# Two transformer blocks on one core: SBUF tiles moved to other offsets within rows of 512 bytes

## The chip, the cores and the metric

The kernel runs on one core of one Trainium2 chip. The metric is device time in microseconds (us) of one execution. The kernel before takes 1174.03 us, the median of two timed runs (1173.64 and 1174.42).

## What is computed

Two blocks over 256 tokens of 1024 features, in float32. The first has two layers (an NSA and a differential attention mixer, then a MoBA mixer, each followed by an MLP), the second an RG-LRU branch beside a forgetting attention, a gated merge and a gated FFN. Cut to the products that take nearly all of the time:

```python
x = x + mixer(rms_norm(x) @ w_in) @ w_out      # layers 0 and 1
x = x + act(rms_norm(x) @ mlp_w1) @ mlp_w2     # 1024 -> 4096 -> 1024
...
proj = h @ w_in_2                              # 1024 -> 7696
y_a = gelu(ga) * rg_lru(conv(xa)); y_b = forgetting_attention(q, k, v, f)
merged = sig(g_a) * (y_a @ w_proj_a) + sig(g_b) * (y_b @ w_proj_b)
x = x + rms_norm(merged @ w_out_2)
up = conv(rms_norm(x) @ w_up)                  # 1024 -> 6144
x = x + rms_norm((gelu(gate) * val) @ w_down)  # 3072 -> 1024
```

## The kernel before, in words

All weights stream in once, in chunks of 1 MB by SyncE's queue (`w_load`, three buffers `raw`). Each chunk holds two units of 128 x 1024. A unit is split into a high and a low part, both float32r: ScalarE writes `whi` (L220), VectorE `wlo` = raw - whi (L221), in six buffers each of the pool `wp` (tags `hi` and `lo`, 4096 bytes of a partition). Activations are split the same way (`gh`/`gl`, `oh`/`ol`, `hh`/`hl`, `yh`/`yl`). A product of 128 features by 256 tokens over one k-tile is then three matmuls (`mm3`, L262 to L264): whi by xh, whi by xl, wlo by xh. In them the weights are the stationary operand (128 columns of 4 bytes: 512 bytes of each partition) and the activations stream past (256 columns: 1024 bytes). Only `gen_nat` (L435 to L437) has the roles the other way round: 128 tokens of `gh` or `gl` stand, and 256 columns of `whi` or `wlo` stream. All these matmuls are 128x128 by 128x256.

Four generators give the order of the work: `gen_pair` (two column tiles over eight k-tiles, from `gh`/`gl`), `gen_nat`, `gen_half` (four k-tiles, from `oh`/`ol`) and `gen_deep` (16, 24 or 32 k-tiles in a row, from `yh` or `hh`). `weave` lays the attention and RG-LRU steps between them. The order is fixed at build time; it runs in program order on each engine.

Where a tile lies in SBUF follows from the order of the `tile()` calls: the pools `cp` (constants), `xp`, `np`, `rawp`, `wp` stand one after the other at the start of the memory, and the pools of a stage (`ap0`, `hp`, `ap1`, `mp`, `fp`, `ff`) on top of them, opened and closed as a stack. Addresses are padded to 32 bytes. As a row k of a streamed tile is 1024 bytes long and a row k of a weight unit 512 (or 1024), the address modulo 512 is the same for every k. Built, the two programs have these offsets (address modulo 512) for the operands of the float32r matmuls, "distance" being the streamed one minus the standing one, modulo 512:

| stage (streamed, standing) | matmuls | before: offsets, distance | after: offsets, distance |
|---|---|---|---|
| `gen_pair` (gh/gl, whi/wlo), the FFN's first product apart | 3744 | 384, 320: 64 | 256, 0: 256 |
| the FFN's first product `w_up` (gh/gl, whi/wlo) | 1152 | 384, 320: 64 | 256, 0: 256 |
| `gen_nat` (whi/wlo, gh/gl) | 528 | 320, 384: 448 | 0, 256: 256 |
| layer 0's output `gen_half` (oh/ol) | 192 | 416, 320: 96 | 0, 0: 0 |
| second product of both MLPs (hh/hl) | 1536 | 320, 320: 0 | 128, 0: 128 |
| layer 1's output (oh1/ol1) | 192 | 320, 320: 0 | 384, 0: 384 |
| `w_pa` (yh/yl) | 240 | 320, 320: 0 | 192, 0: 192 |
| `w_pb` (oh2/ol2) | 192 | 320, 320: 0 | 320, 0: 320 |
| the FFN's second product (hh2/hl2) | 576 | 320, 320: 0 | 0, 0: 0 |

Two small products have standing units of 24 and 16 columns (`gen_small`: NSA's gates and the forget logits, `gs` in the profile). In the second the k-th unit stands at offset 320 + 64 k modulo 512, and `gh`/`gl` stream at 384, so its distances go 64, 0, 448, 384, 320, 256, 192 and 128.

Of the kernel before, what the change touches and what calls it, by code (L numbers as in the profile page):

```python
# [7 lines left out]
F32 = mybir.dt.float32  # L8
# [50 lines left out]
def kernel(  # L59
# [29 lines left out]
    cp = ctx.enter_context(tc.tile_pool(name="cp", bufs=1))  # L89
    xp = ctx.enter_context(tc.tile_pool(name="xp", bufs=1))  # L90
    np_ = ctx.enter_context(tc.tile_pool(name="np", bufs=2))
    rawp = ctx.enter_context(tc.tile_pool(name="rawp", bufs=3))
    wp = ctx.enter_context(tc.tile_pool(name="wp", bufs=6))
# [8 lines left out]
    ones = cp.tile([128, 128], F32, name="ones")  # L102
    mhalf = cp.tile([128, 8], F32, name="mhalf")
    x = xp.tile([128, KT, T], F32, name="x")
    gh = xp.tile([128, KT, T], FR, name="gh")
    gl = xp.tile([128, KT, T], FR, name="gl")
# [14 lines left out]

# [1 line left out]
    chunks = []  # L123
# [47 lines left out]
    add_stream(w_dn, U8)  # L171

    W = Ctl()
    W.raw = []
# [54 lines left out]

    # orders of k for a start on two pairs at once: unit by unit for a few k, or k by k  # L230
    K422 = ((0, 1, 2, 3), (4, 5), (6, 7))
# [4 lines left out]
    def w_next(held=0):  # L236
        # held: units taken whose products are not yet issued
        while len(W.q) < min(1 + AHEAD, 6 - held):
            if not w_split():
                break  # L240
        return W.q.pop(0)
# [4 lines left out]

# [1 line left out]
    def bc(ap, n):  # L248
# [48 lines left out]
    class Norm:  # L297
        # sums of squares over the features; the last `tail` tiles go straight to the summing products
        def __init__(self, t1=3, t2=6, tail=0):
# [146 lines left out]
    def gen_deep(ntile, nu, xh, xl, evac, group=1):  # L446
        # the first `group` column tiles are worked on unit by unit
        def block(js):
            pss_ = {j: psg.tile([128, 2, T], F32, tag="g", name="g") for j in js}
            for u in range(nu):  # L450
                for j in js:
                    wh, wl, (nk, ncol) = w_next()
                    if j == ntile - 1 and u == nu - 1:
                        w_ahead(4)
                    for k in range(nk):
                        kk = u * nk + k
                        mm3(pss_[j][:, 0, :], wh[:, k, :], wl[:, k, :], xh[:, kk, :], xl[:, kk, :], kk == 0, kk == nu * nk - 1)
                        if k == nk // 2 - 1:
                            tick()
                            yield  # L460
                    if u == nu - 1:
                        evac(j, pss_[j][:, 0, :])
                    tick()
                    yield

        yield from block(range(group))
        for j in range(group, ntile):
            yield from block([j])
# [87 lines left out]

# [1 line left out]
    BT = 3  # L558
# [3 lines left out]
    def maps_gen(maps, ap):  # L562
# [5 lines left out]
        def A(n):  # L568
            if n % 2 == 0:
                # two heads side by side, on the upper and the lower rows of the array  # L570
                qs = []
                for i in (n, n + 1):
                    m = maps[i]
                    if m.get("pre"):
                        m["pre"]()
                    st[i] = pss.tile([128, 512], F32, tag="s", name="s")
                    qs.append((st[i], m["q"](), m["k"]()))
                for s, q, k in qs:
                    nc.tensor.matmul(out=s[:, 128:384], lhsT=q[:, 128:256], rhs=k, start=True, stop=True)  # L579
                for s, q, k in qs:  # L580
                    nc.tensor.matmul(out=s[:, 0:128], lhsT=q[:, 0:128], rhs=k[:, 0:128], start=True, stop=True)
            m, s = maps[n], st[n]
# [84 lines left out]
    def pv_cols(S, n, v0, v1, first):  # L667
        # value product of one head, feature-major: rows of head n % 2, pair n // 2
        def f(ps):
# [7 lines left out]

# [1 line left out]
    xv = xT.rearrange("k p t -> p k t")  # L679
# [14 lines left out]
    w_load()  # L694
    tb_t = cp.tile([33, 16], F32, name="tb_t")
    nc.vector.memset(tb_t[32:33, :], NEGB)
    nc.vector.memset(ones, 1.0)
    nc.vector.memset(mhalf, -0.5)
    warm = cp.tile([128, 8], F32, name="warm")
    nc.scalar.activation(out=warm, in_=mhalf, func=AF.Square)  # L700
    # the tensor engine's clock rises with use: keep it busy until the first weights are here
    wps = pst.tile([128, 512], F32, tag="t", name="wps")
# [24 lines left out]

# [1 line left out]
    bias_ctx = ExitStack()  # L729
# [49 lines left out]

# [1 line left out]
    A0 = ExitStack()  # L781
    ap0 = A0.enter_context(tc.tile_pool(name="a0", bufs=1))
    qT = ap0.tile([128, 4, T], F32, name="qT")
    ksT = ap0.tile([128, T], F32, name="ksT")
# [14 lines left out]
    nlam = ap0.tile([128, 1], F32, name="nlam")  # L799
    wcmp = [ap0.tile([128, 2048], F32, tag="e8", name="wcmp%d" % i, bufs=2) for i in range(2)]  # L800
    for i in range(2):
        nc.sync.dma_start(out=wcmp[i], in_=w_cmp[i])

    norm = Norm(*(4, 7))
# [89 lines left out]
    def compress_gen():  # L894
# [16 lines left out]
        yield  # L911
        # keys on rows 0..29, values on rows 64..93
        hz = ap0.tile([94, 128], F32, name="hz")
# [3 lines left out]
        hp = pss.tile([128, 512], F32, tag="s", name="hp")  # L917
# [32 lines left out]

    # position n of the head order (i, g) -> head g * 4 + i
    HORD = [(n % 2) * 4 + n // 2 for n in range(8)]
# [126 lines left out]

    # the first sums of squares, in tiles that are free so far  # L1080
    sqs = [qT[:, 0:2, :], qT[:, 2:4, :], kcd[:, :, 0:T], vcd[:, :, 0:T]]
# [7 lines left out]
    norm.tail = 3  # L1089
    sgain = cp.tile([128, 1], F32, name="sgain")  # L1090
    have = {}
# [57 lines left out]

# [1 line left out]
    def mlp(norm, gain_next, nrm, nrm2=None):  # L1151
        st = ExitStack()
        hp = st.enter_context(tc.tile_pool(name="hp", bufs=1))
        hh = hp.tile([128, 32, T], FR, name="hh")
        hl = hp.tile([128, 32, T], FR, name="hl")
# [17 lines left out]
    def log1pe(pool, z, n, pre):  # L1173
        # log(1 + exp(-|z|)) by 2 atanh(e / (2 + e)); returns the steps and the result
        e = pool.tile([128, n], F32, name=pre + "e")
# [26 lines left out]

# [1 line left out]
    A1 = ExitStack()  # L1204
    ap1 = A1.enter_context(tc.tile_pool(name="a1", bufs=1))
    rb8 = ap1.tile([128, T], F32, name="rb8")
    vn = ap1.tile([128, 2, D], F32, name="vn")
    oh = ap1.tile([128, KT, T], FR, name="oh1")
    ol = ap1.tile([128, KT, T], FR, name="ol1")
# [57 lines left out]
    )  # L1267
    nsp = cp.tile([128, 10], F32, name="nsp")
    psp = cp.tile([128, 10], F32, name="psp")
    hb = cp.tile([128, 20], F32, name="hb")  # L1270
    hm = cp.tile([128, 16], F32, name="hm")
    sp_steps, sp_q = log1pe(cp, V("lam"), 10, "sp")
# [18 lines left out]

# [1 line left out]
    gc = cp.tile([128, 8], F32, name="gc")  # L1293
    nc.vector.tensor_tensor(out=gc, in0=V("fin"), in1=V("pre2"), op=ALU.mult)
# [3 lines left out]
    M = ExitStack()  # L1298
    mp = M.enter_context(tc.tile_pool(name="mp", bufs=1))
    yh = mp.tile([128, 10, T], FR, name="yh")  # L1300
    yl = mp.tile([128, 10, T], FR, name="yl")
# [38 lines left out]

# [1 line left out]
    RG = ExitStack()  # L1342
# [56 lines left out]
    def rg_gen():  # L1399
        for half in range(2):  # L1400
# [5 lines left out]
            for o in range(5):  # L1406
# [3 lines left out]
                for m in range(2):  # L1410
                    # blocks off the diagonal reach at most half of the columns
                    nb = [(pi, slice(0, 64) if pi < o else slice(64, 128)) for pi in prs if pi != o]
# [32 lines left out]
    def evac_f(ps):  # L1445
# [14 lines left out]
        def st15():  # L1460
            # log_sigmoid(z) = min(z, 0) - log(1 + exp(-|z|))
            nc.vector.scalar_tensor_tensor(out=L.l, in0=zn, scalar=0.0, in1=L.l, op0=ALU.min, op1=ALU.subtract)
# [32 lines left out]

# [1 line left out]
    FA = ExitStack()  # L1497
    fp = FA.enter_context(tc.tile_pool(name="fp", bufs=1))
    oh = fp.tile([128, KT, T], FR, name="oh2")
    ol = fp.tile([128, KT, T], FR, name="ol2")  # L1500
# [75 lines left out]

# [1 line left out]
    PO = ExitStack()  # L1578
# [34 lines left out]

# [1 line left out]
    FF = ExitStack()  # L1615
# [83 lines left out]

# [1 line left out]
def _pack(w, groups):  # L1701
# [226 lines left out]
```

## Time and profile before

| | us |
|---|---|
| median of the timed runs | 1174.03 |
| the profiled execution, first to last instruction (its span) | 1170.4 |
| left around the span, as median minus span | 3.7 |
| TensorE busy in the span | 1138.5 (97%) |
| VectorE busy | 793.4 (68%) |
| ScalarE busy | 625.7 (53%) |

The float32r matmuls above are 8352 of the 9343 matmul records. The time that the profile gives for one matmul (some 280 ns) is from its start to the end of its passage through the array, and follows overlap: what a matmul costs in a row of them is the distance from its start to the next one's start. That is read from the timeline, or from a stretch of known length and the number of matmuls in it (the count includes the two or three that are still under way as the stretch opens). The weight load of the next matmul runs during the present one.

### The profile page before, as it was taken

Reading aid. Unit: us, or ns where it says so; the run is one execution under the profiler, and the core shown is the slowest. Engines: PE = TensorE matmul, PEld = TensorE weight load, DVE = VectorE, ACT = ScalarE, POOL = GpSimd, SP = SyncE. Lnnn points to the kernel's source line nnn. Section 1 sums busy time; section 2 is a strip of 40 time slices with the busy share of each in tenths; the row PEclk is TensorE's granted clock in tenths of the full one; section 3 lists DMA queues with packets and bytes.
Section 4 is the critical chain, followed back from the end, with each engine's and each line's share of the span. In section 5 each row is a group of like instructions: output and inputs, shape, how many; then the busy total and the mean of one; then the engine's idle time right before and its main releaser. Section 6 shows DMA issues by size and latency. Waiting matters only on the chain.

```text
span 1170.4 us, 22694 instructions
## 1 busy us (share of the span) xinstructions
PE 1138.5 (97%) x9343; PEld 1088.1 (93%) x9343; DVE 793.4 (68%) x1404; ACT 625.7 (53%) x1112; POOL 190.3 (16%) x228
## 2 busy tenths in 40 slices
PE   8999999999999999999999999999999999999996
PEld 7987799999999889999999897999999999999996
DVE  5767766674545777566445787766567689999842
ACT  4346555653444545565434577644454556676641
POOL 2014320000010123000001000042310123222211
PEclk9999999999999999999999999999999989999998
DMA  8832244555444334355455453564555525445641
GB/s 331 290 136 73 74 180 145 212 202 199 177 184 180 141 113 145 144 214 206 158 215 198 153 204 109 175 239 141 166 180 197 173 99 167 164 175 180 212 149 36
DMA packets 31303, 200.01 MB, mean 171 GB/s; under 512 B 3594, under 2 KB 6042, under 8 KB 9056
## 3 DMA queue, kind: packets, MB, share of 16 engines
q1 hardware_dynamic: 28832, 187.23, 44.6%
q0 software_dynamic: 2080, 11.08, 2.9%
q8 instruction: 73, 1.20, 0.4%
q14 instruction: 30, 0.25, 0.1%
q10 hardware_dynamic: 288, 0.26, 0.1%
HBM read 197.43 MB, written 3.22 MB: 171 GB/s over the span
## 4 chain that ended last, share of the span: by engine, by line
PE 78%; DVE 14%; ACT 3%; issue 2%; POOL 2%; DMA 1%; SPq 0%; POOLq 0%; ACTq 0%
PE g L262 22%; PE g L264 21%; PE g L263 21%; DVE y L1643 4%; DVE wlo L221 4%; PE rgp L1414 2%; PE g L435 2%; PE g L436 2%; PE g L437 2%; PE pt L623 1%; PE o L673 1%; DVE u L1631 1%; ACT whi L220 1%; PE s L579 1%; DVE y L1655 1%
## 5 line engine op out<-in xcount | busy, mean ns | idle before, releaser
L221 DVE TENSOR_TENSOR wlo<-raw,whi 128x1024 fp32r<-128x1024 f32 (+2 forms) x356 | 420.3, 1212 | 114.2 <-ACT whi L220 113.9
L262 PE MATMUL g<-gh,whi 128*128 128x256 f32 x1632 | 463.7, 284 | 3.2 <-ACT whi L220 1.7
L264 PE MATMUL g<-gh,wlo 128*128 128x256 f32 x1632 | 460.1, 282 | 3.1 <-DVE wlo L221 3.1
L263 PE MATMUL g<-gl,whi 128*128 128x256 f32 x1632 | 457.6, 280 | 0.5 <-DVE gl L257 0.4
L220 ACT CAST whi<-raw 128x1024 fp32r<-128x1024 f32 (+2 forms) x356 | 349.9, 1024 | 18.0 <-PE g L263 8.4
L262 PEld LDWEIGHTS g<-gh,whi 128*128 128x128 f32 x1632 | 309.1, 189 | 10.6 <-issue 5.4
L264 PEld LDWEIGHTS g<-gh,wlo 128*128 128x128 f32 x1632 | 309.2, 189 | 7.2 <-DVE wlo L221 7.1
L263 PEld LDWEIGHTS g<-gl,whi 128*128 128x128 f32 x1632 | 309.4, 190 | 1.1 <-DVE gl L257 0.7
L262 PE MATMUL g<-hh,whi 128*128 128x256 f32 x704 | 199.4, 283 | 1.3 <-DVE u L1631 1.3
L264 PE MATMUL g<-hh,wlo 128*128 128x256 f32 x704 | 199.3, 283 | 0.2 <-DVE wlo L221 0.2
L263 PE MATMUL g<-hl,whi 128*128 128x256 f32 x704 | 199.2, 283 | 0.0
L262 PEld LDWEIGHTS g<-hh,whi 128*128 128x128 f32 x704 | 135.1, 192 | 1.5 <-ACT q L1652 1.5
L264 PEld LDWEIGHTS g<-hh,wlo 128*128 128x128 f32 x704 | 135.1, 192 | 0.4 <-DVE wlo L221 0.4
L263 PEld LDWEIGHTS g<-hl,whi 128*128 128x128 f32 x704 | 135.1, 192 | 0.0
L317 POOL TENSOR_TENSOR acc<-acc,sq 128x256 f32<-128x256 f32 x53 | 42.4, 806 | 465.2 <-ACT sq L313 464.3
L612 POOL TENSOR_TENSOR p<-p,rr 128x384 f32<-128x384 f32 x56 | 50.1, 895 | 205.9 <-DVE rr L607 92.8
L597 ACT ACTIVATE p<-p,nm 128x256 f32<-128x256 f32 x112 | 49.9, 448 | 56.0 <-DVE nm L588 55.8
L1643 DVE SCALAR_TENSOR_TENSOR y<-u,cw,y 128x255 f32<-128x255 f32 (+1 forms) x96 | 60.1, 685 | 0.0
L262 PE MATMUL g<-oh,whi 128*128 128x256 f32 x192 | 55.6, 290 | 0.0
L264 PE MATMUL g<-oh,wlo 128*128 128x256 f32 x192 | 54.3, 283 | 0.0
L263 PE MATMUL g<-ol,whi 128*128 128x256 f32 x192 | 54.2, 282 | 0.0
L1160 ACT ACTIVATE u<-u 128x512 f32<-128x512 f32 x32 | 20.2, 632 | 61.9 <-DVE u L1159 61.9
(317 smaller groups left out, 1455.8 us busy)
## 6 DMA issues: line engine op xcount, KB each, us to landing
raw<-in_w_in_dram SPq DMA_DIRECT2D x30, 1024.0 KB, 4.9
raw<-in_w_up_dram SPq DMA_DIRECT2D x24, 1024.0 KB, 4.9
raw<-in_w_m1a_dram SPq DMA_DIRECT2D x16, 1024.0 KB, 4.8
raw<-in_w_m2a_dram SPq DMA_DIRECT2D x16, 1024.0 KB, 5.0
raw<-in_w_m1b_dram SPq DMA_DIRECT2D x16, 1024.0 KB, 4.9
raw<-in_w_m2b_dram SPq DMA_DIRECT2D x16, 1024.0 KB, 4.9
raw<-in_w_od_dram SPq DMA_DIRECT2D x12, 1024.0 KB, 4.8
raw<-in_w_dn_dram SPq DMA_DIRECT2D x12, 1024.0 KB, 4.8
```

The source lines that it names most:

```text
L220: nc.scalar.copy(out=hi[:, a:b], in_=t[:, off + a:off + b])
L221: nc.vector.tensor_tensor(out=lo[:, a:b], in0=t[:, off + a:off + b], in1=hi[:, a:b].bitcast(F32), op=ALU.subtract)
L262: nc.tensor.matmul(out=o, lhsT=wh, rhs=xh, start=start, stop=False, skip_group_check=skip)
L263: nc.tensor.matmul(out=o, lhsT=wh, rhs=xl, start=False, stop=False, skip_group_check=skip)
L264: nc.tensor.matmul(out=o, lhsT=wl, rhs=xh, start=False, stop=stop, skip_group_check=skip)
L317: nc.gpsimd.tensor_tensor(out=self.acc, in0=self.acc, in1=dst, op=ALU.add)
L435: nc.tensor.matmul(out=ps[:, b, :], lhsT=xh[:, k, bs], rhs=wh[:, k % 4, :], start=(k == 0), stop=False)
L436: nc.tensor.matmul(out=ps[:, b, :], lhsT=xh[:, k, bs], rhs=wl[:, k % 4, :], start=False, stop=False)
L437: nc.tensor.matmul(out=ps[:, b, :], lhsT=xl[:, k, bs], rhs=wh[:, k % 4, :], start=False, stop=(k == KT - 1))
L597: nc.scalar.activation(out=p[:, c0:c1], in_=p[:, c0:c1], func=AF.Exp, scale=-1.0, bias=nm[:, b:b + 1], accum_out=sm[:, b:b + 1],)
L612: nc.gpsimd.tensor_tensor(out=pv, in0=pv, in1=w, op=ALU.mult)
L1643: nc.vector.scalar_tensor_tensor(out=y[:, a, d:], in0=u[:, a, 0:T - d], scalar=cw[:, w, c:c + 1], in1=y[:, a, d:], op0=ALU.mult, op1=ALU.add)
```

## The change

Tiles move; nothing else does. A helper `pad` allocates a tile of n floats per partition that no instruction touches, and it is called at seven places (once per MLP in `mlp`), ahead of the tiles named in the diff. Eight small tiles of the pool `cp` and the two `wcmp` tiles are allocated earlier than they were, so that what follows them starts at the wanted offsets. Comments are taken out, which moves line numbers by up to 17 (L262 of before is L279 after). The programs have the same instructions, in the same order, on every engine; a few POOL instructions wait for other semaphores, of transfers that ended long before. The highest address in use goes from 227,200 to 228,096 bytes.

```diff
+    pads = []
+
+    def pad(pool, n):
+        pads.append(0)
+        pool.tile([128, n], F32, tag="pad%d" % len(pads), name="pad", bufs=1)
+
...
     mhalf = cp.tile([128, 8], F32, name="mhalf")
+    tb_t = cp.tile([33, 16], F32, name="tb_t")
+    warm = cp.tile([128, 8], F32, name="warm")
+    sgain = cp.tile([128, 1], F32, name="sgain")
+    nsp = cp.tile([128, 10], F32, name="nsp")
+    psp = cp.tile([128, 10], F32, name="psp")
+    hb = cp.tile([128, 20], F32, name="hb")
+    hm = cp.tile([128, 16], F32, name="hm")
+    gc = cp.tile([128, 8], F32, name="gc")
+    pad(xp, 32)
     x = xp.tile([128, KT, T], F32, name="x")
+    pad(xp, 64)
     gh = xp.tile([128, KT, T], FR, name="gh")
     gl = xp.tile([128, KT, T], FR, name="gl")
...
+    pad(wp, 16 + 64)
     W = Ctl()
...
     ap0 = A0.enter_context(tc.tile_pool(name="a0", bufs=1))
+    wcmp = [ap0.tile([128, 2048], F32, tag="e8", name="wcmp%d" % i, bufs=2) for i in range(2)]
     qT = ap0.tile([128, 4, T], F32, name="qT")
...
         hp = st.enter_context(tc.tile_pool(name="hp", bufs=1))
+        pad(hp, 32)
         hh = hp.tile([128, 32, T], FR, name="hh")
...
     vn = ap1.tile([128, 2, D], F32, name="vn")
+    pad(ap1, 96)
     oh = ap1.tile([128, KT, T], FR, name="oh1")
...
     mp = M.enter_context(tc.tile_pool(name="mp", bufs=1))
+    pad(mp, 48)
     yh = mp.tile([128, 10, T], FR, name="yh")
...
     fp = FA.enter_context(tc.tile_pool(name="fp", bufs=1))
+    pad(fp, 32)
     oh = fp.tile([128, KT, T], FR, name="oh2")
```

## Rows read from the trace of the kernel before

**Rows 1.** The page, busy time of each engine and granted TensorE clock in 40 slices.
```profile
PE 1138.5 (97%) x9343; PEld 1088.1 (93%) x9343; DVE 793.4 (68%) x1404; ACT 625.7 (53%) x1112; POOL 190.3 (16%) x228
...
PEclk9999999999999999999999999999999989999998
```

**Rows 2.** What PE waited for longest: us in total, times, longest.
```profile
PE pt L623 <- POOL p L612: 5.4, 7, 1.3
PE g L264 <- DVE wlo L221: 3.3, 18, 0.4
```

**Rows 3.** The page, costliest groups: line, engine, operation, count | busy us, mean ns | idle before.
```profile
L262 PE MATMUL g<-gh,whi 128*128 128x256 f32 x1632 | 463.7, 284 | 3.2 <-ACT whi L220 1.7
...
L262 PE MATMUL g<-hh,whi 128*128 128x256 f32 x704 | 199.4, 283 | 1.3 <-DVE u L1631 1.3
```

**Rows 4.** Windows: us from the span's start, length, busy us and (xcount) per engine, PEclk.
```profile
186.00:240.00 54.00, 54.00 (x479) 54.00 (x478) 37.61 (x42) 32.88 (x42) 0.00 (x0) 1.00 0.58 202
486.00:540.00 54.00, 54.00 (x461) 54.00 (x460) 37.79 (x42) 31.55 (x40) 0.00 (x0) 1.00 0.56 196
765.00:780.00 15.00, 15.00 (x130) 15.00 (x129) 9.67 (x8) 7.58 (x9) 10.72 (x10) 1.00 0.81 281
250.00:304.00 54.00, 54.00 (x453) 54.00 (x452) 27.18 (x30) 21.74 (x29) 2.23 (x3) 1.00 0.53 196
550.00:604.00 54.00, 54.00 (x452) 54.00 (x451) 26.12 (x29) 21.77 (x31) 4.33 (x6) 1.00 0.52 196
890.00:908.00 18.00, 18.00 (x152) 18.00 (x152) 16.80 (x25) 7.41 (x11) 0.00 (x0) 1.00 0.63 226
1100.00:1140.00 40.00, 40.00 (x336) 40.00 (x335) 18.69 (x17) 18.35 (x27) 5.40 (x6) 1.00 0.51 185
682.00:704.00 22.00, 22.00 (x197) 22.00 (x196) 18.85 (x32) 15.53 (x23) 0.38 (x1) 1.00 0.61 222
960.00:1080.00 120.00, 117.03 (x960) 113.70 (x959) 118.61 (x182) 82.78 (x140) 34.42 (x40) 1.00 0.49 166
```

**Rows 5.** Timeline of PE in the first MLP's second product (first of 15 rows, and last).
```profile
264.75 0.28 PE L263 MATMUL g<-hl,whi 128*128 128x256 f32 x1
...
266.43 0.28 PE L262 MATMUL g<-hh,whi 128*128 128x256 f32 x1
```

**Rows 6.** The chain of waits, two successive pairs of the FFN's first product: start us, us, what.
```profile
1034.66 1.35 DVE y L1643 x3
1040.76 1.35 DVE y L1643 x3
```

**Rows 7.** Timeline of PE in the forget-logit product: 16 standing columns, k from 0 on.
```profile
712.10 0.29 PE L262 MATMUL gs<-gh,whi 128*16 128x256 f32 x1
712.23 0.28 PE L263 MATMUL gs<-gl,whi 128*16 128x256 f32 x1
712.35 0.28 PE L264 MATMUL gs<-gh,wlo 128*16 128x256 f32 x1
712.46 0.28 PE L262 MATMUL gs<-gh,whi 128*16 128x256 f32 x1
712.58 0.28 PE L263 MATMUL gs<-gl,whi 128*16 128x256 f32 x1
712.70 0.28 PE L264 MATMUL gs<-gh,wlo 128*16 128x256 f32 x1
...
713.16 0.28 PE L262 MATMUL gs<-gh,whi 128*16 128x256 f32 x1
...
714.63 0.28 PE L263 MATMUL gs<-gl,whi 128*16 128x256 f32 x1
```

**Rows 8.** VectorE's unit split in two stages: 244 to 338 us, then 486 to 540 us.
```profile
L221 DVE TENSOR_TENSOR wlo<-raw,whi 128x1024 fp32r<-128x1024 f32 x35 | 40.6, 1221 | 5.8 <-ACT whi L220 5.8
...
L221 DVE TENSOR_TENSOR wlo<-raw,whi 128x1024 fp32r<-128x1024 f32 x22 | 26.0, 1223 | 2.8 <-ACT whi L220 2.8
```

More of the change, by code (lines that the diff above doesn't have):

```diff
@@ L694 @@
     w_load()
-    tb_t = cp.tile([33, 16], F32, name="tb_t")
     nc.vector.memset(tb_t[32:33, :], NEGB)
@@ L698 @@
     nc.vector.memset(mhalf, -0.5)
-    warm = cp.tile([128, 8], F32, name="warm")
     nc.scalar.activation(out=warm, in_=mhalf, func=AF.Square)
@@ L799 @@
     nlam = ap0.tile([128, 1], F32, name="nlam")
-    wcmp = [ap0.tile([128, 2048], F32, tag="e8", name="wcmp%d" % i, bufs=2) for i in range(2)]
     for i in range(2):
@@ L1089 @@
     norm.tail = 3
-    sgain = cp.tile([128, 1], F32, name="sgain")
     have = {}
@@ L1267 @@
     )
[L1268 to L1271, printed above, removed]
     sp_steps, sp_q = log1pe(cp, V("lam"), 10, "sp")
@@ L1290 @@
     bias_ctx.close()
-    gc = cp.tile([128, 8], F32, name="gc")
     nc.vector.tensor_tensor(out=gc, in0=V("fin"), in1=V("pre2"), op=ALU.mult)
```

## Prediction

> **What bounds the kernel now.** I read the page first. TensorE is busy 97% of the span and its clock is granted in full, 2.4 GHz, in nearly every slice [rows 1]; so the question is what one matmul costs, not what it waits for. The waits confirm it: the longest of PE's, for `p` and for `wlo`, sum to 5.4 and 3.3 us [rows 2]. The groups give 1632 matmuls per line from `gh`/`gl` and 704 from `hh`/`hl`, all of one shape [rows 3].
>
> Next come windows, laid where nothing but these matmuls run, and here the reader is to look at the counts. In 54 us the first MLP's first product starts 479, the second MLP's same product 461, and the second products of both 453 and 452 [rows 4]. Less the two or three that are under way as a window opens, that is 113.3, 117.8 and 120.0 ns from start to start. The timeline says the same: 14 distances from 264.75 to 266.43 us, 120.0 ns each [rows 5]. Same instruction, same clock, no idle time, three prices. I then set the prices beside the table of offsets, stage by stage. At distance 0 every stage costs 120: both MLPs' second products, `w_pb` (152 in 18 us), the FFN's second product (336 in 40 us) [rows 4]. At distance 64 a stage costs 117.8 or, after some interruptions and until the next, 113.3, as in 682 to 704 us (197 in 22 us) [rows 4]. Going through all start times, the 4272 `gh`/`gl` matmuls outside the FFN (distances 64 and 448) run at 113.3 in three of ten cases and else at 117.8; their mean is 0.31 x 113.3 + 0.69 x 117.8 = 116.4. No matmul of this kind starts its next in less than 113 ns, so I call 113.3 the floor.
>
> One stage is bound otherwise. In the FFN's first product, 960 to 1080 us, VectorE is busy 118.6 of 120 us and PE 117.0 [rows 4], and the chain of waits runs through the convolution on VectorE, pair after pair, 6.1 us apart [rows 6]. There VectorE sets the pace.
>
> **The change part by part.** It adds no instruction and takes none away, so the whole effect is the price per matmul at a new distance. The step I choose is what distances 128 to 384 cost; no stage has them now. From below the bound is the floor, 113.3. From above it is 120.0, the dearest stage. Which of them is nearer? The forget-logit product is the one place where such distances occur, for a load of 16 columns. For k = 0 to 2 (distances 64, 0, 448) its matmuls start irregularly, 712.10 to 713.16 us, nine in 1.06 us or 117.8 ns each, the first with 130. From k = 3 on (384, 320, 256, 192, 128) they are even: 713.16 to 714.63 us, 13 in 1.47 us, 113.1 ns as rounded, which is the floor [rows 7]. A clash of the first line of the load with the first of the stream, which an offset of 128 or more avoids, would look like this. I take the floor for 128 to 384. The weak point: 16 columns are an eighth of a load, and a load of 128 columns sweeps all 512 bytes of a row while the stream sweeps it twice.
>
> The sum, in the profiled execution:
> - `gh`/`gl` outside the FFN and `gen_nat`: seven of ten go from 117.8 to 113.3. 4272 x 0.69 x 4.45 ns = 13.1 us, less the one in 25 that follows a wait: 12.6. These stages are woven with attention and RG-LRU; I take off a tenth for work that then ends later than PE would like (`p` on POOL is late already [rows 2]): 11.3 us.
> - `hh` of both MLPs, 1536 from 120.0 to 113.3: 10.2 us. PE has no idle time there, and VectorE is half busy, 27.2 of 54 us [rows 4], so it comes through whole.
> - `oh1`, `yh`, `oh2`, 624 of them, same step: 4.2 us, less the waits in the woven ones: 3.8.
> - `oh` goes from 96 to 0. It costs 120 now by its start times and 120 after. The FFN's second product stays at distance 0: 0 us for 576.
> - The FFN's first product, 1152 from 117.8 to 113.3, would be 5.1 us, but VectorE hides it; I take 0. If that cover were thinner than it looks, at most PE's idle part of the stretch tells: VectorE's own slack is 1.4 of 120 us [rows 4], so 1.6 us over 24 pairs.
> - Operands of VectorE, ScalarE and POOL move too. Their price at other offsets is not in the trace; the split takes 1221 ns in one stage and 1223 in another [rows 8], so I take 0, with 1.5 us either way, which in the FFN's first product would reach the end.
>
> Together 25.3 us less. The span is 1170.4 and the median of the runs 3.7 above it; added as they are, 1174.0 - 25.3 = 1148.7, say 1149. Within this case 1145 to 1154: the tenth I took off may be nothing (-1.3) or three tenths (+2.6), and 1.5 us either way. What is late next is VectorE's split of the weights in the first products, 37.8 of 54 us [rows 4], which has room.
>
> A rule speaks against all of this. The Trainium skill, SBUF — State Buffer, section "Who interferes with whom", says that TensorE has two read ports of its own, one for the streamed operand and one for the weight load, and that "PE and ACT never wait on anyone". By that rule offsets cannot matter and the sum is 0, the last rival below. The trace differs with it where one form of product passes through several offsets: in the forget-logit product the price settles from 117.8 to 113.1 as the offset moves on [rows 7].
>
> **The rivals.**
> - *A clash cannot be avoided at a general distance (slower).* The stream passes a row of 512 bytes twice while the load passes it once, so they meet once per matmul wherever they start, unless the meeting falls into the gap between two matmuls; distances 64 and 448 then are the lucky ones, next to that gap. For it: 113.3 occurs only there, and distance 0 is always at 120. Against it: the even rows from k = 3 on [rows 7]. It decides from the first matmul at distance 256 that keeps 120: 4272 x 0.96 x (120 - 116.4) = 14.8 us more, `hh` and the rest unchanged: 1189. The FFN's first product adds nothing, as 48 x 120 ns = 5.8 us a pair still fit into VectorE's 6.1 [rows 6].
> - *Something between.* Distances of 128 and more behave as 64 does, two prices and mostly the dearer. Then `gh`/`gl` stay as they are and 2160 matmuls go from 120 to 116.4: 7.5 us, 1167. Near it lie the mixed cases, one of 128 and 256 good and the other bad: 1162 with 256 alone good, 1175 with 128 alone.
> - *The offsets have nothing to do with it*, and the stage's form sets the price: 1174. For it: the price changes at one distance without any change of address, 479 against 461 [rows 4], and form and offset go together before, as 64 occurs in `gen_pair` alone and 0 in `gen_deep` and `gen_half` alone. Against it: the matmuls themselves are the same in all of these [rows 3], and in the forget-logit product the form stays while the price settles [rows 7].
>
> **How the numbers follow.** The forecast, floor at all new distances, gets 0.40; between and mixed 0.26; slower 0.26; no effect 0.08. The predicted time is 1149, its own range 1145 to 1154. For 8 in 10 the range must take in the cases between, 1160 to 1176, and most of the slower one, so it goes from 1146 to 1189; that leaves out a little at either end. 2% of 1174.0 is 23.5 us, about what a measurement of this kernel can tell from no change: faster by that means below 1150.5, which some six in ten of the forecast's cases reach: 0.24. Slower means above 1197.5; no case has it but errors in several terms: 0.02. Within 2%: 0.74.
>
> **What would show it.** Right, if the counts in 54 us of the MLPs' products all read about 479, first and second product alike, while the FFN's second product still reads 336 in 40 us and its first product keeps VectorE at 98%. Wrong in the main step, if `gh`/`gl` at distance 256 read 461 or 452 in 54 us; wrong in the second, if `hh` at 128 still reads 452. Wrong in the cover, if the FFN's first product gets shorter than 6.1 us a pair. Wrong altogether, if every stage reads as before.

## The result, and the profile after

The changed kernel takes 1182.43 us (two runs, 1182.40 and 1182.45) against 1174.03: a ratio of 1.0076 with a 95% interval of 1.0047 to 1.0105. It is 8.4 us slower; that is less than 2%, and clearly not the 25 us faster of the forecast. The profiled execution's span is 1180.6 us, 10.2 more than before.

Three lines of the page of the kernel after answer to [rows 1] and [rows 3].

```profile
PE 1150.1 (97%) x9343; PEld 1100.4 (93%) x9343; DVE 794.7 (67%) x1404; ACT 625.4 (53%) x1112; POOL 189.9 (16%) x228
...
L279 PE MATMUL g<-gh,whi 128*128 128x256 f32 x1632 | 470.1, 288 | 4.1 <-ACT whi L237 2.6
...
L279 PE MATMUL g<-hh,whi 128*128 128x256 f32 x704 | 198.6, 282 | 1.3 <-DVE u L1644 1.3
```

PE is busy 11.6 us longer with the same 9343 matmuls, and VectorE, ScalarE and POOL are where they were, within 1.3 us. The `gh` group went from a mean of 284 to 288 ns, `hh` from 283 to 282. So the time came in through the price of a matmul, and in the wrong group.

The windows of the kernel after, laid in the same stages as [rows 4]. The columns are the same: stretch, length, then busy time and count for PE, PEld, DVE, ACT and POOL.

```profile
190.00:244.00 54.00, 54.00 (x452) 54.00 (x452) 36.95 (x42) 31.50 (x40) 0.00 (x0) 1.00 0.55 196
492.00:546.00 54.00, 54.00 (x452) 54.00 (x452) 36.98 (x42) 31.51 (x40) 0.00 (x0) 1.00 0.54 195
255.00:309.00 54.00, 54.00 (x457) 54.00 (x457) 26.44 (x29) 20.79 (x28) 2.20 (x3) 1.00 0.52 196
556.00:610.00 54.00, 54.00 (x458) 54.00 (x457) 26.79 (x28) 23.03 (x32) 4.31 (x6) 1.00 0.51 193
900.00:918.00 18.00, 18.00 (x155) 18.00 (x154) 16.82 (x25) 7.71 (x10) 0.00 (x0) 1.00 0.63 218
1110.00:1150.00 40.00, 40.00 (x335) 40.00 (x334) 19.00 (x17) 18.66 (x27) 5.39 (x6) 1.00 0.51 185
970.00:1090.00 120.00, 118.85 (x960) 115.78 (x960) 118.61 (x181) 82.72 (x141) 34.37 (x40) 1.00 0.49 166
```

The first two windows are the first products of the two MLPs, `gh`/`gl` at distance 256. Before, they read 479 and 461 matmuls in 54 us; now both read 452, which was the mark of 120 ns. The next two are the second products, `hh` at distance 128: 457 and 458, where 452 stood before and 479 was forecast. `w_pb` (distance 320) has 155 instead of 152. The FFN's second product stayed at distance 0 and reads 335 instead of 336. The last window is the FFN's first product: 960 matmuls in 120 us as before, while PE is busy 118.85 us instead of 117.03.

A piece of PE's timeline in the first MLP's first product (start, duration, engine, operation; 13 rows lie between the two):

```profile
194.75 0.28 PE L281 MATMUL g<-gh,wlo 128*128 128x256 f32 x1
...
196.43 0.28 PE L280 MATMUL g<-gl,whi 128*128 128x256 f32 x1
```

From the first start to the last are 14 steps in 1.68 us, 120.0 ns each, just as [rows 5] showed for distance 0.

The prices of the float32r matmuls, worked out from the start times in the two traces (each matmul whose successor starts within 131 ns), and what these cost above 113.33 ns each, stage by stage:

| stage | distance before, after | mean ns before, after | us above the floor, before, after |
|---|---|---|---|
| gh/gl, the FFN's first product apart | 64, 256 | 116.4, 119.8 | 11.1, 23.5 |
| gen_nat | 448, 256 | 116.6, 119.9 | 1.7, 3.4 |
| hh, both MLPs | 0, 128 | 120.0, 118.7 | 10.2, 8.2 |
| oh1 | 0, 384 | 119.8, 118.4 | 1.2, 0.9 |
| yh | 0, 192 | 119.7, 114.8 | 1.4, 0.3 |
| oh2 | 0, 320 | 120.0, 117.8 | 1.3, 0.9 |
| oh (layer 0) | 96, 0 | 119.7, 119.7 | 1.2, 1.2 |
| hh2 | 0, 0 | 119.9, 120.0 | 3.8, 3.8 |
| sum | | | 31.8, 42.1 |

The table gives 10.3 us more, the span 10.2. The FFN's first product is left out of it: from the start of its first matmul to that of its last it takes 147.4 us before and 147.5 after.

### The profile page after: what moved, and what is told of

It reads as the page before. It is cut to its first block, busy times and chain, and to the rows that moved or that the text cites. A ratio compares the mean times of both kernels' runs of the same rounds, so it can differ in the third digit from the quotient of the medians.

```text
span 1180.6 us, 22693 instructions
## 1 busy us (share of the span) xinstructions
PE 1150.1 (97%) x9343; PEld 1100.4 (93%) x9343; DVE 794.7 (67%) x1404; ACT 625.4 (53%) x1112; POOL 189.9 (16%) x228
## 4 chain that ended last, share of the span: by engine, by line
PE 79%; DVE 14%; ACT 2%; issue 2%; POOL 2%; DMA 1%; SPq 0%; POOLq 0%; ACTq 0%; DVEq 0%
PE g L279 22%; PE g L280 21%; PE g L281 21%; DVE y L1656 4%; DVE wlo L238 4%; PE rgp L1426 2%; PE g L452 2%; PE g L453 2%; PE g L454 2%; PE pt L640 1%; PE o L690 1%; DVE u L1644 1%; PE s L596 1%; ACT whi L237 1%; DVE y L1668 1%
## 5 line engine op out<-in xcount | busy, mean ns | idle before, releaser
L238 DVE TENSOR_TENSOR wlo<-raw,whi 128x1024 fp32r<-128x1024 f32 (+2 forms) x356 | 421.2, 1214 | 116.4 <-ACT whi L237 116.1
L279 PE MATMUL g<-gh,whi 128*128 128x256 f32 x1632 | 470.1, 288 | 4.1 <-ACT whi L237 2.6
L281 PE MATMUL g<-gh,wlo 128*128 128x256 f32 x1632 | 466.1, 286 | 1.2
L280 PE MATMUL g<-gl,whi 128*128 128x256 f32 x1632 | 464.5, 285 | 0.5 <-DVE gl L274 0.4
L279 PEld LDWEIGHTS g<-gh,whi 128*128 128x128 f32 x1632 | 315.4, 193 | 11.5 <-issue 5.7
L281 PEld LDWEIGHTS g<-gh,wlo 128*128 128x128 f32 x1632 | 315.2, 193 | 4.9 <-DVE wlo L238 4.9
L280 PEld LDWEIGHTS g<-gl,whi 128*128 128x128 f32 x1632 | 315.4, 193 | 1.1 <-DVE gl L274 0.7
L279 PE MATMUL g<-hh,whi 128*128 128x256 f32 x704 | 198.6, 282 | 1.3 <-DVE u L1644 1.3
L279 PEld LDWEIGHTS g<-hh,whi 128*128 128x128 f32 x704 | 133.2, 189 | 1.5 <-ACT q L1665 1.5
L279 PE MATMUL g<-oh,whi 128*128 128x256 f32 x192 | 55.3, 288 | 0.0
```

The source lines that it names most:

```text
L238: nc.vector.tensor_tensor(out=lo[:, a:b], in0=t[:, off + a:off + b], in1=hi[:, a:b].bitcast(F32), op=ALU.subtract)
L279: nc.tensor.matmul(out=o, lhsT=wh, rhs=xh, start=start, stop=False, skip_group_check=skip)
L280: nc.tensor.matmul(out=o, lhsT=wh, rhs=xl, start=False, stop=False, skip_group_check=skip)
L281: nc.tensor.matmul(out=o, lhsT=wl, rhs=xh, start=False, stop=stop, skip_group_check=skip)
```

## The experiments

The theory after the result: a product's price goes by where its stream stands to the load of the next weights, and 256 is as bad as 0. Rivals: the price goes with the absolute place of the weights or the stream; the other tiles that the change moved cost the time; the stage's form sets the price. A ratio is to runs of the kernel before that were taken beside the run in question; their medians are 1172.4 us for `gh64`, `shift192` and `all192`, 1174.7 for `all192b` and `all112`, and 1174.5 for `hh112` and `hh196`.

**The price by distance, by itself (`scan`).** Both blocks are left out. Bursts of 48 float32r products, 128 standing and 256 streamed columns, three bursts to a case, with a short pause ahead of each.

```diff
+    for d, wo in CASES:
+        o = ((wo + d) % 512) // 4
+        c = wo // 4
...
+                nc.tensor.matmul(
+                    out=ps[:, 0:256], lhsT=w[:, c + k * 128:c + k * 128 + 128], rhs=s[:, o + k * 256:o + k * 256 + 256],
+                    start=i == 0, stop=i == 48 - 1,
+                )
```

> Leaves the two blocks out: only bursts of 48 float32r matmuls 128x128 by 128x256, three bursts per case, each after one small float32 matmul that ends the steady row; the tile name gives distance d and weight offset w in bytes. Distance theory: the start-to-start time is a function of d modulo 256 alone: 120 ns at d = 0 and 256, 118 to 119 at 128 and 384, 113.3 or 117.8 at 64, 192, 320 and 448, the same at every w; at d off multiples of 32 the stream starts inside a 64-byte piece and costs 120. Rival, absolute place: prices at equal d differ by more than 2 ns between w = 0, 64, 128, 192, 256, 320 and 384. Rival, distance with a period of 512: d and d + 256 differ.

Four cases of `scan`: the answer for a tile gives shortest, median and longest duration, then first and last start.

```profile
L118 PE MATMUL d000w000x<-s,w x144: 277/283/365, 17.0 to 34.7; 128*128 128x256 f32 x144
...
L118 PE MATMUL d112w000x<-s,w x144: 275/275/365, 140.7 to 157.5; 128*128 128x256 f32 x144
...
L118 PE MATMUL d256w000x<-s,w x144: 277/283/365, 299.0 to 316.6; 128*128 128x256 f32 x144
...
L118 PE MATMUL d368w000x<-s,w x144: 275/275/365, 422.6 to 439.5; 128*128 128x256 f32 x144
```

Distances 0 and 256 take 17.7 and 17.6 us from the first start to the last, 112 and 368 take 16.8 and 16.9. Nothing else runs here, so neither another engine nor the stage's form is needed for the two prices. The steady price in ns (from start times, the first ten products of a burst left out; several numbers where the three bursts differ; d and d + 256 gave the same):

```
  0: 120.0               64: 117.8 / 113.3       128: 120.0 / 118.7 / 118.6   192: 113.3
 16: 118.7/116.6/113.4   80: 120.1 / 119.9       144: 118.8 / 118.7 / 116.7   208: 119.0
 32: 116.7 / 117.8       96: 120.0               160: 118.6                   224: 118.3
 48: 118.4              112: 113.3 (all bursts)  176: 119.2                   240: 117.2
```

With the weights at 32 to 384 instead of 0, distance 0 stayed at 120.0 and 64 at 117.8 or 113.3; 192 gave 113.3 in all bursts but two of the three with the weights at 64 and two of the three with them at 320. So the period is 256, not 512, and the floor is the exception: most distances cost 116 to 120. The expectation held for the period and for the place of the weights. It missed at distances that are no multiple of 32, which are not all at 120 (112 is at the floor, 240 at 117.2), and at 128, where some bursts cost 120.0.

**The changed kernel with `gh`/`gl` back at distance 64 (`gh64`).** The weights stay at multiples of 512, and all else of the change stays.

```diff
-    pad(xp, 64)
+    pad(xp, 16)
...
-    pad(wp, 16 + 64)
+    pad(wp, 128)
```

> The changed kernel with gh and gl alone moved back to distance 64 (gen_nat to 448), weights still at multiples of 512. Distance theory: 4272 matmuls go from 119.8 to between 116.4 and 117.8 ns, 8 to 14 us less than the changed kernel: 1168 to 1174 us. Rival, weights at multiples of 512 are dear in themselves: 1182 us as the changed kernel.

1171.93 us, a ratio of 0.9998 to the kernel before (0.9988 to 1.0008). A window of `gh64` in the first MLP's first product:

```profile
190.00:244.00 54.00, 54.00 (x461) 54.00 (x461) 37.20 (x41) 32.39 (x42) 0.00 (x0) 1.00 0.58 206
```

It reads 461, the price of 117.8, where the changed kernel reads 452. Undoing this one distance takes the whole loss away: the other moves of the change are not its cause. It gains nothing on the kernel before, though `hh`, `yh` and `oh2` are cheaper, because `gh`/`gl` now fall into 117.8 more often (mean 117.6 instead of 116.4; all stages together are 31.7 us above the floor, 31.8 before the change).

**The kernel before with everything 192 bytes on, distances kept (`shift192`).**

```diff
+    xp.tile([128, 48], F32, tag="pad1", name="pad", bufs=1)
     x = xp.tile([128, KT, T], F32, name="x")
```

> The kernel before with one pad of 192 bytes ahead of x: weights come to multiples of 512, every distance stays. Distance theory: 1174 us, within 3 us for the share of matmuls at 113.3 and 117.8. Rival, the absolute offset of the weights sets the price: up to 1190 us, since all 8352 matmuls would go to 120.

1173.47 us, 1.0013 (1.0004 to 1.0022). Weights at multiples of 512, as in the change, and next to nothing happens: the absolute place is not what costs. The little that is left, 1.3 us in the span, goes with `gh`/`gl` again, whose mean is 117.0 instead of 116.4.

**Every streamed tile at distance 192 (`all192` and, again, `all192b`).** One pad per stage takes another size; `gen_nat` is then at 320.

```diff
-    pad(xp, 64)
+    pad(xp, 48)
...
-        pad(hp, 32)
+        pad(hp, 48)
```

> The changed kernel with every streamed tile at distance 192 (gen_nat at 320). Distance theory with 192 as good as yh was in the changed kernel (mostly 113.3): gh/gl and gen_nat 4272 from 119.8, hh 1536 from 118.7, hh2 576 and oh 192 from 120, the rest from 118: 20 to 35 us less than the changed kernel, 1147 to 1162 us, and at 117.8 throughout 1170 us. Rival, absolute place: within 5 us of 1182.

1157.06 us (1152.52 to 1165.24), 0.9889 (0.9838 to 0.9939). The windows of `all192` for the second products of the first and the second MLP:

```profile
250.00:304.00 54.00, 54.00 (x479) 54.00 (x479) 29.56 (x33) 24.98 (x33) 2.95 (x4) 1.00 0.53 197
560.00:614.00 54.00, 54.00 (x461) 54.00 (x460) 27.69 (x30) 25.01 (x35) 7.14 (x10) 1.00 0.48 176
```

The same instructions at the same distance: 479 in one MLP, 461 in the other. At 192, as at 64, there are two prices.

> The same kernel as all192 (every streamed tile at distance 192, the natural projections at 320), again. If a row's price at this distance is chosen anew in each execution (113.3 or 117.8, as the bursts at 192 show), its times lie spread over some 1150 to 1166 with a median near 1157, and the profile shows other stages at 117.8 than the one before did; if the placement alone decides, the second MLP (hh of the second layer) is again the one at 117.8 and the times agree within 2 us.

1156.02 us (1153.58 to 1158.37), 0.9836 (0.9817 to 0.9855). The second MLP is at 461 again, so that choice comes with the program; but the FFN's first product and layer 0's output were priced otherwise than the first time (means 115.0 and 114.6 ns against 113.8 and 117.2), so some of it is chosen anew in each execution. Neither expectation held alone.

**Finer steps and shorter loads (`scan2`).** As `scan`, with six bursts of 40 to a case.

```diff
+                nc.tensor.matmul(
+                    out=ps[0:nw, 0:ns], lhsT=w[:, c + k * 128:c + k * 128 + nw],
+                    rhs=s[:, o + ks * ns:o + ks * ns + ns], start=i == 0, stop=i == 40 - 1,
+                )
```

> Both blocks are left out; the kernel only loads x and runs bursts of 40 float32r products (standing tiles of 128 columns, streams of 256, unless the name says otherwise), six bursts to a case, each behind a pause of another length; a tile's name gives distance, place of the weights, standing columns (n) and streamed columns (s). Theory A (the load of the next weights and the running stream meet in the SBUF, and the price goes by their distance modulo 256): at 112 and 368 all six bursts are at 113.3 ns, wherever the weights lie; at 192 most are, some at 117.8; 4 or 8 bytes to either side of 112 the price is already above 116. Shorter loads meet the stream for less time: at distance 0 the price falls from 120.0 with 128 standing columns to about 118 with 64 and 114 with 16; a stream of 512 columns pays the same 6 to 7 ns above its floor of 220 as one of 256. Theory B (the price is set by the start of the stream alone, when the load before it has not ended): the price at distance 0 does not fall with fewer standing columns, and at 112 it differs with the place of the weights (32, 64, 128 and so on). Theory C (what made 113.3 at 112 was the burst's phase): of six bursts at 112 two or three are at 117.8, as at 192.

Some cases of `scan2` (n: standing columns, s: streamed columns), shown as for `scan`:

```profile
L119 PE MATMUL d112w064n128s256x<-s,w x240: 275/275/366, 584.9 to 613.4; 128*128 128x256 f32 x120
...
L119 PE MATMUL d116w000n128s256x<-s,w x240: 282/286/368, 135.6 to 166.1; 128*128 128x256 f32 x120
...
L119 PE MATMUL d000w000n064s256x<-s,w x240: 276/276/315, 817.1 to 845.1; 128*64 128x256 f32 x120
L119 PE MATMUL d000w000n016s256x<-s,w x240: 274/276/312, 990.2 to 1018.1; 128*16 128x256 f32 x120
...
L119 PE MATMUL d192w000n016s256x<-s,w x240: 275/280/315, 1046.7 to 1075.5; 128*16 128x256 f32 x120
...
L119 PE MATMUL d112w016n128s256x<-s,w x240: 278/284/368, 1246.1 to 1275.9; 128*128 128x256 f32 x120
```

112 and 368 cost 113.3 to 113.6 ns in all 48 of their bursts with the weights at multiples of 32. Four bytes on, at 116, it is 122.6 to 123.0 (30.5 us instead of 28.5 for 240 products); 4 and 8 bytes before, 117.6 to 120.0. At 192 one burst of six was at 117.8, at 196 all were at 123.0 to 123.5. With weights and stream both moved by 16 bytes, distance 112 costs 118.3 to 120.0, so the difference is not the whole rule.

Fewer standing columns at distance 0: 128 columns 120.0, 96 columns 115.9, 64 and 16 columns 113.3 in all bursts. The stream is the same in these, so the price depends on the load beside it, and not on the start of the stream alone (Theory B). It does not fall evenly: 32 columns gave 120.0, 117.8 and 113.3, and at distance 192 16 columns gave 117.8 in five bursts of six, where 128 columns were at 113.3 in five of six. A load of 16 columns says nothing about one of 128. Theory A's prices for the shorter loads and its 6 to 7 ns above a floor of 220 for a stream of 512 columns were wrong: 512 columns take 226.7 at distance 0, twice 113.3, and 232 to 233 at 128 and 192. Theory C is out, as no burst at 112 was at 117.8.

**One tile pair alone: `hh`/`hl` at 112 and at 196 in the kernel before (`hh112`, `hh196`).** The two kernels differ in the place of `hh` and `hl` by 84 bytes.

```diff
-        hh = hp.tile([128, 32, T], FR, name="hh")
+        hp.tile([128, 24], F32, tag="pad1", name="pad", bufs=1)
+        hh = hp.tile([128, 32 * T + 8], FR, name="hh")[:, 4:4 + 32 * T].rearrange("p (k t) -> p k t", k=32)
```

> The kernel before with one thing changed: hh and hl of both MLPs stand at distances 112 and 368 from the weights instead of 0. Theory A (the price of a product is that of its distance modulo 256 in the bursts, and the MLPs' second products have nothing else in their way): 1536 products from 120.0 to 113.3 ns, 10.2 us less, a ratio of 0.991; the windows in the second products read about 479 matmuls in 54 us, everything else as before. Theory B (a cheaper second product is given back by waits behind it, in the split of the weights or the norm): the same counts in the windows, but less than 7 us of it in the time.

> The same with hh and hl at distances 196 and 452, 84 bytes further and 4 bytes off a distance that is at 113.3 in most bursts. Theory A: the bursts at 196 cost 123.1 to 123.45 ns, so 1536 products are 3.1 to 3.45 ns dearer than before: 4.8 to 5.3 us more, a ratio of 1.004, and about 440 matmuls in 54 us. Rival (the price in the kernel goes by the 32- or 64-byte block in which a tile starts, so that 196 is as 192): 113.3 or 117.8 ns, 3 to 10 us less than before.

`hh112` takes 1164.34 us, 0.9921 (0.9907 to 0.9935), `hh196` 1176.52, 1.0023 (1.0012 to 1.0034). The first MLP's second product, in `hh112`:

```profile
255.00:309.00 54.00, 54.00 (x479) 54.00 (x478) 27.68 (x30) 23.05 (x30) 2.99 (x4) 1.00 0.55 209
```

and in `hh196`:

```profile
255.00:309.00 54.00, 54.00 (x446) 54.00 (x445) 24.03 (x28) 20.42 (x28) 2.94 (x4) 1.00 0.50 188
```

479 against 446 in 54 us, for 84 bytes. `hh112` won 10.1 us in the prices of `hh` (mean 113.4 ns) and 9.3 in the time (0.0079 x 1174.5): it comes through almost whole, as Theory A had it. In the profiled execution `gh`/`gl`, which were not touched, cost 1.6 us more than in that of before, by falling into 117.8 more often; so its span is 8.9 us shorter. At 196 the price was 121.7, dearer than at 0 as expected, but not the 123 of the bursts; that four bytes more than 192 would change nothing is excluded.

**Every streamed tile at 112 or 368 (`all112`).** Each starts 16 bytes into a tile of its own; `gen_nat` is then at 400 and 144.

```diff
+    def off16(pool, k, name, **kw):
+        t = pool.tile([128, k * T + kw.pop("room", 8)], FR, name=name, **kw)
+        return t[:, 4:4 + k * T].rearrange("p (k t) -> p k t", k=k)
...
-    pad(xp, 64)
-    gh = xp.tile([128, KT, T], FR, name="gh")
-    gl = xp.tile([128, KT, T], FR, name="gl")
+    pad(xp, 24)
+    gh = off16(xp, KT, "gh")
+    pad(xp, 56)
+    gl = off16(xp, KT, "gl")
```

> Every streamed tile starts 112 or 368 bytes behind a multiple of 512 (16 bytes into a tile of its own, the second of each pair 256 bytes on), the weights at multiples of 512; where the weights are streamed (the natural projections) the distance is 400 or 144. Theory A (period of 256; at 112 the price is 113.3 in every burst): the steady products of gh, gl, hh, hl, oh, ol, yh, yl cost 113.3 to 113.5 ns throughout, where the kernel at distance 192 still pays 117.8 in many rows; its steady products stood 15.8 us above 113.3 in all in its profiled execution of 1156.4 us, 1.3 of them in the natural projections, which would now pay about 2 to 2.5: some 1143 us, a ratio of 0.975 (0.972 to 0.980). Theory B (VectorE or ScalarE pay for starts that are no multiple of 32 bytes, or become what the products wait for): the prices fall as above, but waits in front of the products grow by what is won, 1150 to 1158. Theory C (the floor at 112 belongs to bursts in which no other engine reads or writes): prices of 117 and more remain and the time stays at that of distance 192, about 1157.

1150.53 us (1149.34 to 1150.85), 0.9792 (0.9778 to 0.9805): faster than both kernels of this case. Its windows: the second products of both MLPs, the FFN's first product and its second.

```profile
255.00:309.00 54.00, 54.00 (x479) 54.00 (x478) 27.69 (x30) 23.04 (x30) 2.99 (x4) 1.00 0.57 210
540.00:594.00 54.00, 54.00 (x479) 54.00 (x478) 28.42 (x31) 26.55 (x38) 5.62 (x8) 1.00 0.56 208
...
940.00:1060.00 120.00, 113.86 (x961) 110.52 (x960) 118.58 (x181) 83.59 (x140) 33.35 (x39) 1.00 0.48 166
1085.00:1125.00 40.00, 40.00 (x356) 40.00 (x355) 19.48 (x17) 20.92 (x30) 4.45 (x6) 1.00 0.50 180
```

All read the floor (356 in 40 us where 336 stood), but for the FFN's first product: 961 matmuls in 120 us, with PE busy only 113.86. What PE waited for in `all112`:

```profile
PE g L286 <- DVE wlo L243: 7.2, 21, 0.6
PE pt L645 <- POOL p L634: 4.7, 6, 1.3
PE nsum L346 <- POOL acc L339: 3.5, 3, 1.2
```

The time is 7.5 us above the expected 1143, and at the edge of what Theory B gave. Three things make up most of the gap. Of what stood above the floor in `all192`, which the expectation took off whole, 0.5 us lay in the FFN's first product, which VectorE paces anyway. Outside of it 7.0 us remain where 2 to 2.5 were expected: `gen_nat` got dearer (119.9 ns, 3.3 us), `gh`/`gl` average 114.0 ns (2.3 us) and the small stages `oh`, `oh1` and `yh` 115.1 to 116.0 (1.3 us). After each interruption a row takes some products to settle: in `gh`/`gl` the first ten cost 115 to 119 ns on average, and from the twelfth on they stand at 113.4. And the wait for `acc` on POOL takes 3.5 us where it took 1.6 in `all192` (2.9 in `all192b`) and 0.8 before. The larger wait for `wlo`, 7.2 us against 3.3 [rows 2], lies for 6.5 us in the FFN's first product and costs nothing there. That VectorE or ScalarE pay for starts off multiples of 32 bytes, the first half of Theory B, does not show: they are busy 792.8 and 625.8 us, 793.4 and 625.7 before.

The terms of all kernels side by side, each from its one profiled execution. "Above the floor" is as in the first table, the FFN's first product left out:

| kernel | us above the floor | span | FFN's first product |
|---|---|---|---|
| before | 31.8 | 1170.4 | 147.4 |
| after | 42.1 | 1180.6 | 147.5 |
| gh64 | 31.7 | 1168.9 | 147.3 |
| shift192 | 33.4 | 1171.7 | 147.2 |
| hh112 | 23.4 | 1161.5 | 147.3 |
| hh196 | 36.7 | 1174.7 | 147.4 |
| all192 | 15.5 | 1154.6 | 147.2 |
| all192b | 14.7 | 1154.7 | 147.2 |
| all112 | 7.0 | 1148.6 | 147.3 |

Against before, the first column changes by +10.3, -0.1, +1.6, -8.4, +4.9, -16.3, -17.1 and -24.8, the span by +10.2, -1.5, +1.3, -8.9, +4.3, -15.8, -15.7 and -21.8. The price explains nearly all of each.

## Why the prediction was wrong

**The step that failed is "I take the floor for 128 to 384".** The new distances cost 119.8 (256), 118.7 (128), 118.4 (384), 117.8 (320) and 114.8 (192). Of the signs that the prediction named, 452 in 54 us for `gh`/`gl` came; `hh`, at 457 and 458, came near its own.

The floor was read off the forget-logit product, 13 even matmuls at 113.1 ns [rows 7]. The prices are there, but what sets them was misread, in two ways. First, those loads have 16 columns, and in the bursts 16 columns cost 113.3 at distance 0 as well, where 128 columns cost 120.0. The prediction named this as its weak point and took the value nonetheless. Second, the price does not settle "as the offset moves on". After the change the same product passes its distances in another order, 256, 192 and 128 first and then 64, 0, 448, 384 and 320. In the kernel after (k = 0, k = 3 and the last):

```profile
721.04 0.29 PE L279 MATMUL gs<-gh,whi 128*16 128x256 f32 x1
...
722.11 0.28 PE L279 MATMUL gs<-gh,whi 128*16 128x256 f32 x1
...
723.70 0.28 PE L281 MATMUL gs<-gh,wlo 128*16 128x256 f32 x1
```

Again the first nine take 1.07 us, 119 ns each, now at the distances that were even before; and the 14 steps from k = 3 on take 1.59 us, 113.6 ns, at 64 and 0 too. So what was read as an effect of the offset came with the later place in the row; where the row settles differs between kernels (in `all192` the same product stays at some 117 ns to its end). The trace of before had a warning as well. NSA's gates are another such product (24 columns, so its distances go 64, 480, 384, 288, 192, 96, 0 and 416), and the forget logits are not the only place where 192 to 384 occur. In the kernel before (k = 0, k = 6 and the last):

```profile
21.68 0.28 PE L262 MATMUL gs<-gh,whi 128*24 128x256 f32 x1
...
23.78 0.28 PE L262 MATMUL gs<-gh,whi 128*24 128x256 f32 x1
...
24.34 0.28 PE L264 MATMUL gs<-gh,wlo 128*24 128x256 f32 x1
```

The first 18 steps, with 384, 288 and 192 among them, take 2.10 us or 116.7 ns each; the last five, at 0 and 416, take 0.56 us, 112 as rounded.

The picture behind the step, first line against first line, fell with it: of the distances tried in a period of 256 only 112 is at the floor in every burst, 16, 64 and 192 are in some, and 4 bytes beside 112 and 192 the price is above 117.

**The terms of the sum.** `gh`/`gl` with `gen_nat`: forecast -11.3, measured +14.1 (23.5 + 3.4 against 11.1 + 1.7). `hh`: forecast -10.2, measured -2.0. `oh1`, `yh`, `oh2`: forecast -3.8, measured -1.8. `oh` and `hh2`, with no gain forecast: right. These make +10.3, and the span says +10.2.

**The slower rival had the sign and the size of the main term.** It kept `gh`/`gl` at 120 at distance 256 and priced that at 14.8 us more; measured are 14.1. It left `hh` and the rest unchanged, which gave 3.8 back, and so came out at 1189 instead of 1182. Its picture is not borne out: it let only distances next to the gap between two matmuls escape, but 112 is at the floor while 48, 80 and 96 around 64 cost 118.4 to 120.1. In both readings the row was taken as 512 bytes long; the bursts show 256, by which distance 256 is distance 0. So its good number for 256 is in part luck. The case between (128 and more as 64) is out for 128 and 256; 320, which is 64 modulo 256, does cost what 64 costs.

**The cover was right, and it is the best-tested step.** The FFN's first product takes 147.2 to 147.5 us in all nine executions, whether its matmuls cost 119.9 ns (after) or 113.8 (`all192`). The chain of waits in `all112` still has VectorE's convolution at the same pace:

```profile
1004.52 1.35 DVE y L1668 x3
...
1010.62 1.35 DVE y L1668 x3
```

6.1 us a pair, as in [rows 6]; PE's busy time in 120 us moves from 118.85 to 113.86 and the stretch does not move.

**The moved operands of the other engines** were taken at 0. `gh64` bears that out: with them all moved and the matmuls' prices as before in sum, the ratio is 0.9998, and its span differs from before's by 1.5 us. The split of the weights now runs from other offsets; VectorE's busy time went from 793.4 to 794.7 us.

**The rival "no effect" and the rule it stands on.** The Trainium skill, SBUF — State Buffer, section "Who interferes with whom", gives TensorE two read ports of its own and says that it never waits on anyone. The runs differ with what the prediction drew from it, that offsets cannot matter: with every other engine still, the same products cost 113.3 or 120.0 ns by the place of the stream alone. The Trainium skill's same section calls the two ports independent of each other. At distance 0 a shorter load alone took the price from 120.0 to 113.3, so load and stream are not independent in their time.

**The arithmetic.** `all112`, which hits the floor nearly everywhere, won 24.2 us against its own runs of before (1174.72), close to the forecast's 25.3; but that is in part luck. By the table of prices the forecast's three terms give 7.2, 10.2 and 2.9 there, 20.3 together, with `gen_nat` off the floor; layer 0's output and the FFN's second product, which the forecast left as they were, give 4.4 more, and the waits take some back. The `hh` term, alone in `hh112`, came out as summed. So most of what was missing was the right distance. Two of the small sums are off by rounding: VectorE's slack over 24 pairs is 1.7 us rather than 1.6, and 256 alone good gives 1163 rather than 1162.

## What to carry to other kernels

Where TensorE is busy throughout, read the step from start to start in stretches without waits; if the same instruction has several prices at a full clock, set them against the operands' addresses. Measure the price of a placement by a scan with the kernel's own shapes before any tile is moved: a row with a shorter load, however even, does not stand in for it. Where a price changes along a row, look whether it goes with the address or with the place in the row; a second row with another order of addresses tells. A good distance found that way held in the kernel (112 in the uninterrupted stages gave 113.3 to 113.5 ns), while one with two prices (64, 192) can be counted on only for the dearer.

## What was not expected of the hardware

The granted clock was 0.99 over the span in every version of the kernel and 1.00 in each window shown, the upper of its two levels (2.4 GHz), so none of this is the clock. Float32r products of 128 standing and 256 streamed columns cost 113.3 to 123.5 ns by their operands' places in the bursts, a spread of 9%, with a period of 256 bytes. Distance 112 is at the floor in all bursts with the weights at multiples of 32; 4 bytes further it is among the dearest. Many distances are steady, but 64 and 192 have two prices, 113.3 and 117.8, and a row keeps the one it falls into (16, 128 and 144 have several as well). With 512 streamed columns it turns round: distance 0 is at 226.7 and 128 and 192 are dearer. Open is what inside the chip has this period, whether the stream meets the load of the next weights or something else that goes with the load, and why moving weights and stream together by 16 bytes costs the floor.
